# Moving 32 conditioning columns out of the latent attention's heads, and adding their biases eight at a time

## The chip, the cores and the metric

The kernel runs on one core of a Trainium2 chip. The metric is device time in microseconds (us). One core has a matrix engine (TensorE, PE; its weight loads are PEld), a vector engine (VectorE, DVE), an activation engine (ScalarE, ACT), a general engine (GpSimd, POOL), and a queue that issues most transfers (SyncE, SP). Each engine runs its own instructions in the order in which they were queued, and waits on semaphores for the others.

## The reference, cut to what matters

A network of two blocks works on 512 tokens of width 1024, in 32-bit floats. Each of its three layers is steered by a conditioning vector of 6 x 1024 numbers, cut into shifts, scales and gates:

```
c_act = silu(c)
for i in range(2):
    mod = c_act @ w_ada[i] + b_ada[i]            # 1024 x 6144
    sh1, sc1, g1, sh2, sc2, g2 = split(mod, 6)
    h = rmsnorm(x, mix_norm[i]) * (1 + sc1) + sh1
    y = fox_mixer(h) if i == 0 else mla_mixer(h)  # 16 heads each, causal
    x = x + g1 * y
    h = rmsnorm(x, ffn_norm[i]) * (1 + sc2) + sh2
    x = x + g2 * hier_moe(h)                      # 16 experts
mod = silu(c2) @ cond_w + cond_b                  # for the second block
...                                               # convolution, recurrence, PEER experts
```

Both mixers end with an output projection of 1024 x 1024. Nothing but `mod` of the second block needs the third conditioning vector.

## The kernel before

**Conditioning columns.** A vector `mod` is held as 48 columns of 128 numbers (8 columns for each of its six parts). One column is a row block of the transposed weight, 128 x 1024 floats (512 KB), loaded by SP into a tile `ada_w`. One DVE instruction multiplies it by the broadcast `silu` row and sums along the row (line 182, with a short read of the accumulator behind it), and one more DVE instruction adds the bias of that column (queued at line 184, run from line 168, so the profile shows it as L168, 128 x 1). The tiles come from a ring of three buffers in whichever pool `self.ring` names; the generator keeps one tile ahead of the column at work.

The first 16 columns of layer 0 are made at the start. The other 128 (32 of layer 0, 48 of layer 1, 48 of the second block) form one generator, `aside`, made in `run`. `step(n)` takes n columns from it. `heads` calls it: `steps` gives, for each quarter of the 16 heads, the columns taken per head. Before, the first attention takes (3, 4, 4, 8) per head, 76 columns, and the latent attention (2, 2, 2, 7), 52. The row `silu` has one buffer: `silu_row` for the second block (line 152 loads it through SP, line 153 applies the function on ACT) comes when column 80 has been used.

**Attention.** `heads` runs the two attentions alike. Four heads form a quarter; `quart` projects a quarter's queries, keys and values ahead of the heads that use them (`proj_tok`, three matmuls by `mm3`, lines 124 to 126). A head makes scores on PE, then a chain for each of four row blocks: maximum on DVE (L318), exponential on ACT (L321), reciprocal and scaling on DVE (L323, L325), transpose on PE (L334), copy on ACT (L335), and at last the product with the values (L352) whose copy by ACT (L353) ends the head. Two heads are interleaved. In the latent attention POOL also scales and rotates queries and keys (L748, L594 to L599, L772).

**Output projection.** `out_proj` splits the attention's output into a high and a low part (L535, L536), and makes eight chunks: a weight tile (L117 on ACT, L118 on DVE), 24 matmuls, and the update of x on DVE (L551); `then` adds the expert router's work for the chunk before. The expert layer's first weights are requested through SP while this runs.

**Order.** A scheduler at compile time orders each engine's queue by a model of the durations, by priority in the order of the program: what is ready is taken early where an engine has room. Tile pools are stacked from the left or the right of the on-chip memory, and a tile that overlaps an older one waits until that one has been used.

Of the kernel before, what the change touches and what calls it, by code (L numbers as in the profile page):

```python
# [15 lines left out]
OP = mybir.AluOpType  # L16
# [9 lines left out]
class Net:  # L26
    def __init__(self, nc, tc, ctx, A, out, dbg=None):
        self.nc, self.tc, self.ctx, self.A, self.out = nc, tc, ctx, A, out
        self.dbg = dbg or {}
        self.ring, self.more, self.over, self.extra, self.turn, self.ahead = None, None, None, {}, {}, {}  # L30

        self.holds, self.hold = [], None
        ec = ctx.enter_context
        self.cp = ec(tc.tile_pool(name="const", bufs=1))
        self.wp = ec(tc.tile_pool(name="wstream", bufs=1))
        self.xp = ec(tc.tile_pool(name="resid", bufs=1))
        self.sm = ec(tc.tile_pool(name="small", bufs=2))
        self.dram = ec(tc.tile_pool(name="dram", bufs=1, space=bass.MemoryType.DRAM))
        self.ps_acc = ec(tc.tile_pool(name="ps_acc", bufs=1, space=PSUM))
        self.ps = None  # L40
        self.consts()
# [111 lines left out]
        nc.scalar.activation(s, s, AF.Silu)  # L153
        return s

    def ada(self, c, w, mod, cols, how="V", bufs=3, lag=2):

        nc = self.nc  # L160
        V = nc.vector
        mod, bias = mod
        cols = list(cols)
        rs, late = [], []

        def total(to):
            while late and late[0][0] <= to:
                late.pop(0)[1]()  # L168

        for k, i in enumerate(cols):  # L170
            total(k)
            while len(rs) < min(k + bufs - 1, len(cols)):
                r = self.ring.tile([128, D], F32, tag="ada", bufs=bufs, name="ada_w")
                nc.sync.dma_start(out=r, in_=w[cols[len(rs)]])
                rs.append(r)
            r = rs[k]
            m = self.small([128, 1], "ada_t", bufs=8)
            if how[k % len(how)] == "S":
                nc.gpsimd.tensor_tensor(r, r, c, op=OP.mult)
                late.append((k + lag, functools.partial(nc.scalar.activation, r, r, AF.Copy, accum_out=m)))  # L180
            else:
                V.scalar_tensor_tensor(r, r, 1.0, c, op0=OP.mult, op1=OP.mult, accum_out=m)  # L182
            e = slice(i, i + 1)
            late.append((k + lag, functools.partial(V.tensor_tensor, mod[:, e], bias[:, e], m, op=OP.add)))
            if k == len(cols) - 1:
                total(k + lag)
            yield

    def step(self, n):
        for _ in range(n):  # L190
            next(self.aside)


# [161 lines left out]
    def heads(self, quart, oT, pool, steps, early, first):  # L355

        nc = self.nc
        ready, run = [], []  # L360

        pt = pool.tile([128, 13, 128], F32, name="pt")

        def fill():
            for q in range(4):
                yield from quart(q, ready)
            while True:
                yield

        self.ring = pool  # L370
        more = fill()
        while not ready:
            next(more)
            next(first, None)
        for _ in first:
            pass
        for _ in range(early):
            next(more)
        for head in range(16):
            r0 = (head % 2) * 64  # L380
            run.append(self.head(ready.pop(0), oT[r0:r0 + 64, head // 2, :], pt, pool))
            last = head == 15
            for k in range(4 if not last else 12):
                for g in reversed(list(run)):
                    if next(g, run) is run:
                        run.remove(g)
                if k != 3:
                    next(more)
                n = steps[head // 4]
                self.step((k + 1) * n // 4 - k * n // 4 if k < 4 else 0)  # L390
            while not ready and not last:
                next(more)
        self.ring = None
# [47 lines left out]
    def fox_heads(self, h, oT, keep, pool):  # L441
        nc, A = self.nc, self.A
        cq = keep.tile([128, 4, 512], BF16, name="f_cq")
        ck = keep.tile([128, 4, 512], BF16, name="f_ck")
# [67 lines left out]

            return score, v[:, :, hh * 64:(hh + 1) * 64]

        self.heads(quart, oT, pool, (3, 4, 4, 8), 1, self.fox_cum(h, cq, ck, oT[:, 2:8], keep))

    def proj_tok(self, ps, h, ws, i):

# [19 lines left out]

    def out_proj(self, x, oT, w, g1, pool, then=None):

        nc = self.nc
        o = self.split(oT, pool, "o")
        for c in range(8):
            wt = self.weight(w[c])
            ps = self.psum("acc", 2)
            for kd in range(8):
                e = slice(kd * 128, (kd + 1) * 128)
                self.mm3(ps, (wt[0][:, e], wt[1][:, e]), (o[0][:, kd, :], o[1][:, kd, :]), kd == 0, kd == 7)
            if then and c:
                then(c - 1)  # L550
            nc.vector.scalar_tensor_tensor(x[:, c, :], ps, g1[:, c:c + 1], x[:, c, :], op0=OP.mult, op1=OP.add)  # L551
        if then:
            then(7)

# [171 lines left out]
    def mla_heads(self, lat, cs, oT, pool):  # L726
        nc, A = self.nc, self.A
        V = nc.vector
        cq, ckv, gq, gk, kss, kr, rest = lat
# [60 lines left out]

            return score, vs[:, :, hh * 64:(hh + 1) * 64]

        self.heads(quart, oT, pool, (2, 2, 2, 7), 2, rest)


    def first_max(self, x, n, k, pool, name):
# [386 lines left out]
    def mla_layer(self, x, mod, cs, stack, then):  # L1183

        with self.pool("m_o") as po:
            oT = po.tile([128, 8, 512], F32, name="oT")
            with self.pool("m_lat") as pl:
                with stack, self.room:
                    lat = self.mla(x, cs, oT, pl)
                with self.pool("m_heads") as p:  # L1190
                    self.mla_heads(lat, cs, oT, p)
            self.cond.close()
            with self.pool("m_out") as p:
                self.out_proj(x, oT, self.A["mla_w_out"], mod[:, 16:24], p, then=then())


    def add_sums(self, sums, x, c, n):
# [612 lines left out]
    def peer_pick(self, h, keep, pool, ahead):  # L1810
# [21 lines left out]
        first = pool.tile([128, 16], BF16, name="first")  # L1832
        step = pool.tile([128, 16], F32, name="step")
        nc.gpsimd.memset(step, 0.0)
        for r0, n, w, at in self.CAND:
            for r in range(r0, r0 + n):
# [323 lines left out]
    def run(self):  # L2160
        nc, A = self.nc, self.A
        self.cond = contextlib.ExitStack()
        cond = self.cond.enter_context(self.pool("cond", "right"))
        act = self.silu_row(A["c"], cond)
        x = self.xp.tile([128, 8, 512], F32, name="x")
        nc.sync.dma_start(out=x, in_=A["x"])
        gain = self.xp.tile([128, 4, 8], F32, name="gain")
        nc.gpsimd.dma_start(out=gain, in_=A["norms"])
        gm, gf = gain[:, 0:2], gain[:, 2:4]
        bias = self.bias = self.xp.tile([128, 3, 48], F32, name="bias")  # L2170
        nc.scalar.dma_start(out=bias, in_=A["b_ada"])
        mods = [self.xp.tile([128, 48], F32, name=f"mod{k}") for k in range(3)]

        def aside():
            for k in range(3):
                c = self.silu_row(A["c2"], cond) if k == 2 else act
                yield from self.ada(c, A[f"w_ada{k}"], (mods[k], bias[:, k]), range(0 if k else 16, 48))

        self.aside = aside()
        loads = [self.moe_loads(l) for l in range(2)]  # L2180
        with self.psum_pool("ps") as self.ps:
            stack = [contextlib.ExitStack() for _ in range(2)]
            start = [functools.partial(self.moe_begin, stack[l], x, gf[:, l], mods[l], loads[l]) for l in range(2)]
            self.fox_layer(x, gm[:, 0], act, mods[0], start[0])
            self.moe_layer(0, x, gf[:, 0], mods[0], lambda room: self.mla_begin(room, x, gm[:, 1], mods[1]))
            self.mla_layer(x, mods[1], self.cs, stack[0], start[1])
            self.moe_layer(1, x, gf[:, 1], mods[1], lambda room: self.second_begin(x))
            self.room.close()
            stack[1].close()
            mod = mods[2]  # L2190
            self.second_mix(x, mod)
        self.peer_layer(x, mod)
# [107 lines left out]
```

## Time and profile before

| | us |
|---|---|
| median of 3 runs | 3050.35 (3048.65 to 3057.16) |
| the profiled execution, device time | 3048.28 |
| its span, first to last instruction | 3046.4 |
| PE busy | 2748.0 (90%) |
| DVE busy | 2342.8 (77%) |
| ACT busy | 1400.3 (46%) |
| POOL busy | 1235.6 (41%) |

Busy times are sums over the whole span; stages differ, so they are read by stretches. [...] In a timeline a line is start, duration, engine, source line, operation, output from input, and in brackets how long the engine was idle before it and what ended that.

### The profile page before, as it was taken

What the parts mean: (1) busy time and instruction counts of PE and PEld (TensorE: products, weight loads), DVE (VectorE), ACT (ScalarE), POOL (GpSimd) and SP (SyncE); (2) the same over time, 40 slices, a digit from 0 to 9 for tenths busy, and PEclk for the clock granted to TensorE, in tenths of its full rate; (3) what the DMA queues carried; (4) which work ended last, traced back from release to release, by engine and by line L of the source; (5) the groups of instructions that cost most, each with busy time, mean ns of one, the idle gap of its engine ahead of it and who ended that gap; (6) DMA issues with size and microseconds to landing.
All of it is one profiled execution on the core that took longest, in us unless ns stands there. A gap on an engine that the chain in (4) does not pass through costs nothing.

```text
span 3046.4 us, 42674 instructions
## 1 busy us (share of the span) xinstructions
PE 2748.0 (90%) x14989; PEld 2234.8 (73%) x14989; DVE 2342.8 (77%) x4500; ACT 1400.3 (46%) x2688; POOL 1235.6 (41%) x894
## 2 busy tenths in 40 slices
PE   2899978898889798899898899999899999999996
PEld 2777556676556566576676588999889999998885
DVE  7998457768974686777974699998598888886667
ACT  3354437744554574432333533688533333333332
POOL 3111017743211484004941245120177777774332
PEclk9999889999899799998998999999999999999998
DMA  6776158933634797221011124796699999997782
GB/s 217 245 231 198 42 212 293 330 132 125 190 126 151 244 341 241 90 73 28 5 59 57 69 83 128 228 316 219 214 363 350 351 356 351 349 351 270 247 265 98
DMA packets 234337, 627.53 MB, mean 206 GB/s; under 512 B 33180, under 2 KB 95948, under 8 KB 230648
## 3 DMA queue, kind: packets, MB, share of 16 engines
q1 hardware_dynamic: 134416, 434.54, 42.0%
q0 software_dynamic: 45120, 154.42, 14.4%
q10 hardware_dynamic: 54568, 35.66, 4.0%
q8 instruction: 122, 2.00, 0.3%
q14 instruction: 111, 0.91, 0.1%
HBM read 564.94 MB, written 63.37 MB: 206 GB/s over the span
## 4 chain that ended last, share of the span: by engine, by line
PE 47%; DVE 13%; DMA 3%; issue 2%; ACT 1%; POOL 0%; POOLq 0%; DVEq 0%; ACTq 0%; SPq 0%
PE acc L124 7%; PE acc L125 7%; PE acc L126 7%; PE y L126 6%; PE y L125 6%; PE y L124 5%; DVE s_y L1367 1%; DMA wraw<-in_moe_w_gu_dram 1%; PE S L1922 1%; PE tr L1922 1%; DVE wlo L118 1%; DMA wraw<-in_moe_w_dn_dram 1%; DVE s_y L1526 1%; DVE wc L1550 1%; DVE t L1774 1%
## 5 line engine op out<-in xcount | busy, mean ns | idle before, releaser
L118 DVE TENSOR_TENSOR wlo<-wraw,whi 128x1024 fp32r<-128x1024 f32 x442 | 620.2, 1414 | 202.9 <-ACT whi L117 198.7
L117 ACT ACTIVATE whi<-wraw 128x1024 fp32r<-128x1024 f32 (+1 forms) x552 | 576.6, 1050 | 415.8 <-PE acc L125 254.3
L124 PE MATMUL acc<-h_hi,whi 128*128 128x384 f32 (+1 forms) x1328 | 475.8, 359 | 12.2 <-ACT z_out L1962 7.5
L126 PE MATMUL acc<-h_hi,wlo 128*128 128x384 f32 (+1 forms) x1328 | 466.6, 351 | 2.2 <-DVE wlo L118 2.2
L125 PE MATMUL acc<-h_lo,whi 128*128 128x384 f32 (+1 forms) x1328 | 468.1, 353 | 0.0
L118 POOL TENSOR_TENSOR wlo<-wraw,whi 128x1024 fp32r<-128x1024 f32 (+1 forms) x110 | 278.8, 2542 | 325.8 <-ACT whi L117 317.7
L124 PE MATMUL y<-whi,hid_h 128*128 128x512 f32 x768 | 299.8, 391 | 8.0 <-ACT hid_h L2059 8.0
L126 PE MATMUL y<-whi,hid_l 128*128 128x512 f32 x768 | 303.0, 395 | 4.2 <-DVE hid_l L2060 4.2
L125 PE MATMUL y<-wlo,hid_h 128*128 128x512 f32 x768 | 302.4, 394 | 0.0
L1994 POOL DMA_INDIRECT gu<-in_peer_u_dram,e x128 | 196.0, 1531 | 243.2 <-DVE gu L2003 172.5
L124 PEld LDWEIGHTS acc<-h_hi,whi 128*128 128x128 f32 x1328 | 251.5, 190 | 30.4 <-ACT z_out L1962 8.4
L126 PEld LDWEIGHTS acc<-h_hi,wlo 128*128 128x128 f32 x1328 | 251.1, 189 | 16.7 <-DVE wlo L118 2.5
L1994 POOL DMA_INDIRECT gv<-in_peer_v_dram,e x128 | 200.1, 1563 | 155.1 <-DVE stage L1927 105.6
L125 PEld LDWEIGHTS acc<-h_lo,whi 128*128 128x128 f32 x1328 | 251.5, 189 | 15.7 <-issue 0.8
L2059 ACT ACTIVATE hid_h<-hid 128x384 fp32r<-128x384 f32 x128 | 67.1, 524 | 286.6 <-PE y L125 263.5
L2035 DVE SCALAR_TENSOR_TENSOR y<-gv,pz,y 128x1024 f32<-128x1024 f32 x128 | 183.5, 1434 | 0.7 <-DMA gv<-in_peer_v_dram,e 0.6
L182 DVE SCALAR_TENSOR_TENSOR ada_w<-ada_w,silu 128x1024 f32<-128x1024 f32 x138 | 174.3, 1263 | 7.8 <-DMA ada_w<-in_w_ada_dram 7.8
L124 PEld LDWEIGHTS y<-whi,hid_h 128*128 128x128 f32 x768 | 145.0, 189 | 38.0 <-ACT hid_h L2059 8.4
L126 PEld LDWEIGHTS y<-whi,hid_l 128*128 128x128 f32 x768 | 145.1, 189 | 33.9 <-DVE hid_l L2060 4.6
L125 PEld LDWEIGHTS y<-wlo,hid_h 128*128 128x128 f32 x768 | 145.0, 189 | 31.1 <-DVE wlo L118 0.3
L2003 DVE SCALAR_TENSOR_TENSOR gu<-gu,hrow 128x1024 f32<-128x1024 f32 x128 | 162.7, 1272 | 5.4 <-DMA gu<-in_peer_u_dram,e 5.4
L124 PE MATMUL acc<-whi,h_hi 128*128 128x256 f32 x480 | 140.6, 293 | 28.4 <-ACT whi L117 18.7
(671 smaller groups left out, 6231.5 us busy)
## 6 DMA issues: line engine op xcount, KB each, us to landing
ada_w<-in_w_ada_dram SPq DMA_DIRECT2D x144, 512.0 KB
wraw<-in_moe_w_gu_dram SPq DMA_DIRECT2D x128, 512.0 KB
wraw<-in_peer_ut_dram SPq DMA_DIRECT2D x128, 512.0 KB
wraw<-in_peer_v_dram SPq DMA_DIRECT2D x128, 512.0 KB
wraw<-in_moe_w_dn_dram SPq DMA_DIRECT2D x64, 512.0 KB
p_gd<-stage SPq DMA_DIRECT2D x24, 1024.0 KB
gt<-p_gd ACTq DMA_DIRECT2D x16, 1536.0 KB
wraw<-in_fox_w_in_dram SPq DMA_DIRECT2D x24, 512.0 KB
```

What stands on the lines that cost most here:

```text
L117: nc.scalar.activation(hi[:, :w], r[:, :w], AF.Copy)
L118: self.low = eng.tensor_tensor(lo[:, :w], r[:, :w], hi[:, :w].bitcast(F32), op=OP.subtract).ins
L124: mm(out=out, lhsT=l[0], rhs=r[0], start=start, stop=False)
L125: mm(out=out, lhsT=l[0], rhs=r[1], start=False, stop=False)
L126: mm(out=out, lhsT=l[1], rhs=r[0], start=False, stop=stop)
L182: V.scalar_tensor_tensor(r, r, 1.0, c, op0=OP.mult, op1=OP.mult, accum_out=m)
L1367: V.scalar_tensor_tensor(acc[:, c, :], *tap(n), acc[:, c, :], op0=OP.mult, op1=OP.add)
L1922: nc.tensor.matmul(out=pt[:, t * 128:(t + 1) * 128], lhsT=a2[:, b * 4 + t, :], rhs=a1[:, b * 4 + t, :], start=True, stop=True)
L1994: nc.gpsimd.indirect_dma_start(out=u, out_offset=None, in_=src[:, :], in_offset=bass.IndirectOffsetOnAxis(ap=e3[:, k:k + 1], axis=0))
L2003: V.scalar_tensor_tensor(u, u, 1.0, hrow, op0=OP.mult, op1=OP.mult, accum_out=z8[b][:, k % 8:k % 8 + 1])
L2035: V.scalar_tensor_tensor(y3, vs.pop(k), z8[k // 8][:, k % 8:k % 8 + 1], y3, op0=OP.mult, op1=OP.add)
L2059: nc.scalar.activation(hh, hid, AF.Copy)
```

## The change

The columns are taken at other places: (3, 4, 4, 12) per head in the first attention (92 columns), two in each of the first four chunks of its output projection (8), (0, 1, 1, 3) per head in the latent attention (20), and two in each of the first four chunks of its output projection (8). So 32 columns leave the latent heads: 16 go to the last quarter of the first attention's heads, 16 to the two output projections.

With `whole`, the sums of eight columns are collected in one tile of 128 x 8 and their biases added by one instruction: 16 adds in place of 128. Where a stage ends, the last step loads no tile ahead (`prefetch`), so that the ring of one pool holds no column of the next; `out_proj` therefore begins with two loads of its own. The pool `cond`, which holds the `silu` row, is stacked from the left in place of the right, and lives until the latent output projection is done; the ring adds three tiles of 4 KB a partition to the pools of the output projections.

```diff
-    def ada(self, c, w, mod, cols, how="V", bufs=3, lag=2):
+    def ada(self, c, w, mod, cols, how="V", bufs=3, lag=2, whole=False):
...
-            while len(rs) < min(k + bufs - 1, len(cols)):
+            while len(rs) < min(k + (bufs - 1 if self.prefetch else 1), len(cols)):
...
-            m = self.small([128, 1], "ada_t", bufs=8)
+            if whole:
+                if i % 8 == 0:
+                    sums = self.small([128, 8], "ada_s", bufs=3)
+                m = sums[:, i % 8:i % 8 + 1]
+            else:
+                m = self.small([128, 1], "ada_t", bufs=8)
...
-            e = slice(i, i + 1)
-            late.append((k + lag, functools.partial(V.tensor_tensor, mod[:, e], bias[:, e], m, op=OP.add)))
+            if not whole:
+                e = slice(i, i + 1)
+                late.append((k + lag, functools.partial(V.tensor_tensor, mod[:, e], bias[:, e], m, op=OP.add)))
+            elif i % 8 == 7:
+                e = slice(i - 7, i + 1)
+                late.append((k + lag, functools.partial(V.tensor_tensor, mod[:, e], bias[:, e], sums, op=OP.add)))
...
-    def step(self, n):
-        for _ in range(n):
+    def step(self, n, last=False):
+        for k in range(n):
+            self.prefetch = not last or k < n - 1
             next(self.aside)
...
-                self.step((k + 1) * n // 4 - k * n // 4 if k < 4 else 0)
+                self.step((k + 1) * n // 4 - k * n // 4 if k < 4 else 0, last and k == 3)
...
-        self.heads(quart, oT, pool, (3, 4, 4, 8), 1, self.fox_cum(h, cq, ck, oT[:, 2:8], keep))
+        self.heads(quart, oT, pool, (3, 4, 4, 12), 1, self.fox_cum(h, cq, ck, oT[:, 2:8], keep))
...
         o = self.split(oT, pool, "o")
+        self.ring = pool
         for c in range(8):
...
+            if c < 4:
+                self.step(2, c == 3)
             if then and c:
...
-        self.heads(quart, oT, pool, (2, 2, 2, 7), 2, rest)
+        self.heads(quart, oT, pool, (0, 1, 1, 3), 2, rest)
...
-            self.cond.close()
             with self.pool("m_out") as p:
                 self.out_proj(x, oT, self.A["mla_w_out"], mod[:, 16:24], p, then=then())
+        self.cond.close()
...
-        cond = self.cond.enter_context(self.pool("cond", "right"))
+        cond = self.cond.enter_context(self.pool("cond"))
...
-                yield from self.ada(c, A[f"w_ada{k}"], (mods[k], bias[:, k]), range(0 if k else 16, 48))
+                yield from self.ada(c, A[f"w_ada{k}"], (mods[k], bias[:, k]), range(0 if k else 16, 48), whole=True)
```

## Rows read from the trace of the kernel before

**Rows 1.** Windows, all engines, by stage: stretch, length, busy (count), clock, DMA share, GB/s.

```profile
145.00:296.00 151.00, 150.22 (x1027) 120.09 (x1026) 136.99 (x380) 76.58 (x185) 19.48 (x18) 1.00 0.69 224
...
313.00:371.00 58.00, 54.29 (x207) 29.43 (x208) 26.50 (x66) 31.10 (x81) 5.16 (x5) 0.79 0.00 1
375.00:418.00 43.00, 43.00 (x177) 29.60 (x175) 20.83 (x20) 15.28 (x18) 11.87 (x5) 1.00 0.60 207
711.00:757.50 46.50, 34.47 (x156) 26.19 (x154) 43.51 (x111) 21.92 (x51) 18.53 (x13) 0.89 0.43 136
757.50:803.90 46.40, 38.64 (x175) 25.91 (x175) 45.30 (x118) 24.95 (x68) 23.00 (x16) 0.89 0.55 171
803.90:889.90 86.00, 72.56 (x328) 46.27 (x328) 77.84 (x229) 47.00 (x126) 15.35 (x10) 0.88 0.58 183
889.90:934.80 44.90, 40.16 (x192) 22.48 (x192) 19.04 (x54) 26.79 (x74) 0.00 (x0) 0.96 0.25 83
938.00:990.00 52.00, 52.00 (x203) 35.11 (x201) 27.72 (x29) 19.16 (x25) 11.11 (x6) 1.00 0.47 156
```

**Rows 2.** Windows of line 182 alone, columns and accumulator reads: DVE busy (count).

```profile
757.50:803.90 46.40, 17.17 (x25) 0.89 0.55 171
803.90:889.90 86.00, 38.30 (x64) 0.88 0.58 183
```

**Rows 3.** Windows of line 168 alone, bias adds: DVE busy (count), ACT busy (count).

```profile
757.50:803.90 46.40, 5.73 (x13) 0.00 (x0) 0.89 0.55 171
803.90:889.90 86.00, 12.36 (x33) 0.00 (x0) 0.88 0.58 183
```

**Rows 4.** Timelines of POOL and of DVE around 773, latent heads.

```profile
772.14 3.67 POOL L772 TENSOR_TENSOR rk<-rk,qk_r_y 128x1536 f32<-128x1536 f32 x1 [7.06 <-DVE qk_r_y L144]
...
773.19 2.63 DVE L168 TENSOR_TENSOR mod<-bias,ada_t 128x1 f32<-128x1 f32 x1
```

**Rows 5.** Waits of PE from 757.5 to 889.9: us, times, longest.

```profile
PE tr L334 <- DVE P L325: 12.3, 4, 3.6
```

**Rows 6.** ACT timeline: ends of latent heads 3, 10 and 15.

```profile
803.87 0.59 ACT L353 ACTIVATE oT<-pv 64x512 f32<-64x512 f32 x1
...
889.86 0.59 ACT L353 ACTIVATE oT<-pv 64x512 f32<-64x512 f32 x1 [0.37 <-PE pv L352]
...
934.75 0.59 ACT L353 ACTIVATE oT<-pv 64x512 f32<-64x512 f32 x1 [5.03 <-PE pv L352]
```

**Rows 7.** PE timeline: every third matmul of a projection, two widths.

```profile
761.48 0.34 PE L126 MATMUL acc<-whi,lat_l 128*128 128x384 f32 x1
...
762.01 0.34 PE L126 MATMUL acc<-whi,lat_l 128*128 128x384 f32 x1
...
787.10 0.40 PE L126 MATMUL acc<-whi,lat_l 128*128 128x512 f32 x1
...
787.80 0.40 PE L126 MATMUL acc<-whi,lat_l 128*128 128x512 f32 x1
```

**Rows 8.** Line 126 from 803.9 to 889.9: one of the three matmul lines of a projection.

```profile
L126 PE MATMUL acc<-whi,lat_l x24: 336/368/397, 804.2 to 861.6; 128*128 128x512 f32 x12, 128*128 128x384 f32 x12
```

**Rows 9.** DVE groups from 76 to 298: busy us, mean ns, idle before.

```profile
L182 DVE SCALAR_TENSOR_TENSOR ada_w<-ada_w,silu 128x1024 f32<-128x1024 f32 x77 | 94.8, 1231 | 6.8 <-DMA ada_w<-in_w_ada_dram 6.8
...
L168 DVE TENSOR_TENSOR mod<-bias,ada_t 128x1 f32<-128x1 f32 x77 | 10.9, 146 | 0.0
```

**Rows 10.** ACT timeline of the latent attention: function and table load.

```profile
728.14 1.06 ACT L153 ACTIVATE silu<-silu 128x1024 f32<-128x1024 f32 x1 [0.84 <-DMA silu<-in_c_dram]
...
744.90 1.28 ACT L321 ACT_TABLE_LOAD   x1
746.20 0.37 ACT L321 ACTIVATE P<-S,sm_mx 128x128 f32<-128x128 f32 x1
```

**Rows 11.** SP queue: loads of the first expert layer's weights.

```profile
370.56 2.30 SPq L105 DMA_DIRECT2D wraw<-in_moe_w_gu_dram  x5
...
424.09 42.00 SPq L105 DMA_DIRECT2D wraw<-in_moe_w_dn_dram  x2
```

More of the change, by code (lines that the diff above doesn't have):

```diff
@@ L29, in __init__ @@
         self.dbg = dbg or {}
-        self.ring, self.more, self.over, self.extra, self.turn, self.ahead = None, None, None, {}, {}, {}
+        self.ring, self.prefetch, self.more, self.over, self.extra, self.turn, self.ahead = None, True, None, None, {}, {}, {}
         self.holds, self.hold = [], None
@@ L551, in out_proj @@
             nc.vector.scalar_tensor_tensor(x[:, c, :], ps, g1[:, c:c + 1], x[:, c, :], op0=OP.mult, op1=OP.add)
+        self.ring = None
         if then:
```

## The prediction

> **What bounds the kernel now.** I read the windows by stage first, then the windows of the column work alone, the timelines of DVE and POOL in the latent heads, and last the ends of the heads.
>
> In the first attention's steady stretch PE is busy 150.2 of 151.0 us at full clock, with DVE at 137.0 [rows 1]: PE sets the pace, a busy DVE costs nothing. In its last heads, 313 to 371, DVE is busy only 26.5 of 58.0 us, and no column is left there: the scheduler has pulled them all forward. [...] The latent heads are the other way round. From 757.5 to 889.9 DVE is busy 45.3 of 46.4 and 77.8 of 86.0 us, PE 38.6 and 72.6, clock 0.89 and 0.88 [rows 1]. Columns are a large part of that DVE time: 17.2 and 38.3 us for line 182 [rows 2], 5.7 and 12.4 us for the bias adds [rows 3]. Without both, DVE would be busy 22.4 of 46.4 and 27.2 of 86.0. PE does wait for DVE: 12.3 us in four waits for the scaled `P` [rows 5]. The last five latent heads have no columns: PE 40.2 of 44.9, DVE 19.0, clock 0.96 [rows 1].
>
> A bias add is dear in the latent heads. In the first attention one takes 146 ns [rows 9]; at 773.19 one takes 2.63 us, ending with the 3.67 us POOL instruction that began before it [rows 4], and everything queued on DVE behind it waits too. The 46 of [rows 3] cost 18.1 us, 393 ns each.
> [...]
>
> **The change, part by part.**
>
> *Latent heads, second stretch, 803.9 to 889.9.* This holds seven heads, 803.87 to 889.86, and the five that follow end at 934.75 [rows 6]: 12.3 us a head against 9.0. It also holds projections: 12 matmuls of each width on each of three lines [rows 8], so 36 of each. Three of 384 columns take 0.53 us and three of 512 take 0.70 [rows 7]: 6.4 + 8.4 = 14.8 us. Seven heads at 9.0 plus 14.8 are 77.7 us, 8 below the 86.0. Were the projections also to fill PE's idle time as the last five heads show it (4.7 us in five heads, 6.6 in seven [rows 1]), it would be 71, a gain of 15. Which columns leave? Before, 13 run in 757.5 to 803.9 and 32 in this stretch (25 and 64 instructions, two to a column) [rows 2], so 7 run earlier, of 52. The scheduler pulls columns forward as soon as it can, so I expect the 20 that stay to be the first 20, done by about 804, and this stretch to lose its columns wholly. I take 10, between 8 and 15; the low bound is 0, should PE's waits there come from something else.
>
> *First stretch, 757.5 to 803.9.* It keeps most of its columns, but the adds shrink from 13 to one or two, 5 us of DVE in a stretch that is 98% full. Three heads at 9.0 and some 10 us of projections (the other half of a quarter's and a bit) would need 37 of the 46.4, so the gain lies between 0 and 9. I take 4. *Front, 711 to 757.5:* DVE 43.5 of 46.5 [rows 1], again a few adds fewer; 0 to 5, I take 2. The latent heads together: -16, bounds 0 and -29.
>
> *First attention, 16 more columns.* One column costs 1.23 us [rows 9] and its 0.08 us read of the accumulator: 21 us. The 77 bias adds of 10.9 us [rows 9] become nine or ten, which frees some 7 us of DVE in 145 to 296, beside its 14 us of idle time there [rows 1]. So about as much room appears as the new columns need, and part of them will run while PE is the bound, at no cost, hidden by 150.2 us of PE work. I let half of them fall behind 296, in a chain where PE waits for the maximum and the scaling. Eight instructions of 1.23 us, each delaying a chain of two interleaved heads by a third of its length: +3. Bounds 0 and 16 x 1.23 = 20.
>
> *The silu row moves too.* Column 80 now falls into the first attention, so the second row's load and function run there, in the midst of exponentials. The function takes 1.06 us, a table load 1.28 [rows 10]. Before, the function needed no load of its own, since the expert layer had left its table; now one load goes ahead of it and one behind it: 1.06 + 2 x 1.28 = 3.6 us on ACT, which the softmax chain waits for. Taken at +2, for PE has the other head; bounds 0 and 3.6.
> [...]
>
> *Output projections, eight columns each.* PE is busy all of 43.0 and all of 52.0 us, DVE 20.8 and 27.7 [rows 1]. Eight columns add 10.5 us to a DVE with 22 and 24 idle. Weight parts are prepared ahead and the update of x has the next chunk's matmuls as cover, so I take +1 each, +2; bounds 0 and, if each column held PE for its length, 20. Their 4.2 MB of loads go through SP, among the expert weights. A column load that waits for a ring tile holds those weights behind it, and the expert layer's first matmuls wait for them. Cover: from 375 to 418 transfers take 0.60 of the engines for 207 GB/s, so eight loads need 12 us of such time, and 17 are free [rows 1]. Besides, the queue itself stands for up to 42 us from 424.09 with its buffers full [rows 11]. Taken at 0; 12 us a layer if that cover were gone. The loads that begin each output projection wait for no data but memory, and find a DVE with other work; 0. The pool's change of side moves 4 KB from one end to the other: 0, with the same cover if it delays an expert tile. The first attention's saved adds lie under PE's work: 0, at most a gain of the 10.9.
>
> *Sum*, on the profiled execution's 3048.3 (span 3046.4 and 1.9 around it): 3048.3 - 16 + 3 + 2 + 2 = 3039.3. The median of the runs is 2.1 above that execution, so the predicted gain is 9 us on its own base, 11 on the median's. About 0.3%, 9 us, is what a measurement can tell from no change: below 3041.2 is faster, above 3059.5 slower.
>
> **The rivals.** *More:* the latent heads fall to PE's own rate in all three stretches, -26, and the new columns hide, +4: 3026. For it: DVE 32% busy without columns in the second stretch, and a clock of 0.96 where none run. Against it: 20 columns and all of POOL's work stay. *Paid back:* the latent heads wait as much for POOL and for chains between ACT and PE as for DVE, and only the adds' waits go, -4; with +7 for the moved work, 3051. For it: only 12.3 us of PE's waits there name the scaled `P` [rows 5]. Against it: that DVE is 91 to 98% full. *Slower:* the moved columns break the chain in 313 to 371 and PE's clock falls. There 54.3 us of PE at 0.79 [rows 1] are 42.9 at full clock; at 0.50 they are 86, +31, so 3048.3 - 16 + 2 + 2 + 31 = 3067. It decides from a granted clock of about 0.55 there (+24, 3060). Against it: DVE has 31 idle us and transfers stand still. *No move at all:* the scheduler may run the 16 in the PE-bound stretch; that only makes the +3 vanish.
>
> **How the numbers follow.** Forecast, 3031 to 3045: 0.44, of which 0.31 below 3041.2. More: 0.21. Paid back, 3045 to 3059: 0.22. Slower: 0.13. Faster is 0.31 + 0.21 = 0.52, no change 0.13 + 0.22 = 0.35, slower 0.13. The predicted time is 3039; the range, 3020 to 3060, goes down to the more of the latent heads' bounds (-29 and small costs) and up to where the slower case begins.
>
> **What would show it.** In the new profile: the latent heads 4 to 10 take 11 us each or less, with no line 182 in them and a clock above 0.88; DVE there is about a third busy; the bias adds are 16 with a total under 10 us; the first attention's last heads end 2 to 7 us later, with one function and two table loads on ACT among them; the output projections keep PE full, and the first expert matmul comes no later after the projection than before. The prediction is wrong if the columns that stay spread over all latent heads, if the waits for DVE are replaced by waits for POOL, or if the clock in the last heads of the first attention drops.

## The result and the profile after

The changed kernel takes 3096.06 us (median of 4 runs, 3088.87 to 3099.59) against 3049.5 (4 runs, 3046.99 to 3057.16): a ratio of 1.0135 [1.011, 1.016], slower, where 3039 was forecast. The span of its profiled execution is 3093.3 us against 3046.4.

I first set the windows of the new trace beside [rows 1], each stretch cut at the same instructions (end of the same head, the same update of x), but for the front, whose row here begins 6 us earlier in its stage than that of [rows 1]. The stretches are: the first attention's steady part, its last heads, its output projection, the latent attention's front to the end of head 0, heads 1 to 3, 4 to 10 and 11 to 15, and its output projection. Columns as in [rows 1]; clock is the mean granted clock of PE in the stretch, as a share of the full one.

```profile
151.00:303.40 152.40, 152.37 (x1033) 121.70 (x1033) 137.10 (x345) 77.50 (x187) 25.85 (x18) 1.00 0.72 237
319.40:380.50 61.10, 54.00 (x210) 28.75 (x210) 27.95 (x71) 27.42 (x74) 6.14 (x5) 0.78 0.11 36
388.00:431.00 43.00, 43.00 (x168) 29.20 (x167) 23.85 (x34) 10.13 (x13) 0.00 (x0) 1.00 0.51 163
728.00:793.00 65.00, 44.50 (x179) 32.54 (x178) 58.22 (x143) 25.64 (x63) 28.64 (x20) 0.84 0.49 156
793.00:831.00 38.00, 34.14 (x170) 22.86 (x171) 31.29 (x91) 22.03 (x59) 10.52 (x9) 0.96 0.41 124
831.00:913.00 82.00, 73.94 (x336) 46.33 (x335) 44.45 (x140) 48.99 (x132) 13.34 (x10) 0.92 0.05 13
913.00:958.50 45.50, 40.54 (x188) 23.15 (x187) 15.84 (x48) 26.02 (x72) 0.00 (x0) 0.92 0.10 35
962.00:1014.00 52.00, 51.89 (x201) 34.77 (x199) 29.59 (x44) 12.18 (x18) 1.17 (x2) 1.00 0.52 181
```

The latent heads did what was meant: 38.0 and 82.0 us in place of 46.4 and 86.0. The windows of the columns alone (now line 188: DVE busy, count) answer to [rows 2]: none is left behind head 3.

```profile
793.00:831.00 38.00, 12.27 (x18) 0.96 0.41 124
831.00:913.00 82.00, 0.00 (x0) 0.92 0.05 13
```

But the front of that stage grew: from one and the same instruction it takes 65.1 us in place of 52.8. Whole stretches that lie between these rows grew too. The table gives the length of seven stages, from the starts of the same instructions in each kernel's trace; below the first line, the difference to it. **First head**: from the span's start to the copy that ends head 0 of the first attention. **Heads**: from there to the copy of head 15. **Out, router**: to the first copy of gathered rows in the expert layer. **Front**: from the last row of the latent projection to the end of latent head 0. **Latent heads**: to head 15. **Out, router 2**: as the first. **Last**: from the first to the last copy of hidden values in the second block's retrieval experts. What lies between (the experts, the second block) differs by less than 6 us each. Each row is one execution: those of pad96 and held_no_out are the slowest of their ten, those of e1_eights, held_wide, held_wide_mod and pad64 the fastest, so a row tells where the time went, and the medians below how much a kernel takes.

| us | first head | heads | out, router | front | latent heads | out, router 2 | last |
|---|---|---|---|---|---|---|---|
| before | 145.1 | 225.5 | 88.1 | 52.8 | 177.2 | 90.7 | 806.6 |
| **after** | +5.9 | +3.7 | +14.1 | +12.3 | -11.8 | +10.9 | +10.0 |
| e1_eights | +6.4 | -2.4 | +0.4 | +0.5 | +3.8 | -0.2 | +9.6 |
| e2_single | +0.4 | +7.0 | +14.3 | +8.3 | -17.7 | +10.7 | +0.1 |
| e3_no_out | +6.5 | +4.5 | +0.9 | +13.6 | -11.8 | +1.5 | +9.9 |
| e6_out_alone | +6.0 | -0.9 | +15.6 | +13.3 | -14.7 | +10.0 | +11.7 |
| n_no_loads | -0.7 | +9.7 | +13.0 | +10.4 | -21.5 | +9.8 | +3.5 |
| m_ring_two | +1.1 | +2.1 | +0.6 | +9.5 | -13.3 | +0.2 | +5.6 |
| h_held | -0.7 | +4.1 | +0.4 | -5.2 | -12.1 | -0.2 | +0.0 |
| held_again | -0.5 | +7.9 | +0.7 | -3.9 | -15.8 | +0.5 | +3.1 |
| held_wide_mod | +6.3 | -0.7 | +1.0 | -3.8 | -9.2 | -0.8 | +0.5 |
| held_wide | +5.6 | +0.8 | +0.5 | -3.8 | -9.1 | -0.1 | +9.7 |
| held_no_out | +0.7 | +6.8 | +0.5 | -0.1 | -6.7 | -0.5 | +14.4 |
| pad96 | +1.7 | +1.2 | -0.1 | -0.1 | -0.5 | +0.2 | +15.4 |
| pad64 | -0.5 | -0.1 | -0.4 | -1.7 | -2.7 | -0.9 | -0.7 |
| pad32 | -0.3 | +0.5 | +0.2 | -0.2 | -3.0 | -0.2 | +9.0 |

The line of the changed kernel adds up to 45.1 of the 46.9 us between the two spans. Four places lose; each is read in the trace before the runs are told.

**First head.** The SP queue of the changed kernel, then that of the kernel before, as the second quarter's weights come up:

```profile
88.85 20.49 SPq L175 DMA_DIRECT2D ada_w<-in_w_ada_dram  x10
110.88 1.54 SPq L105 DMA_DIRECT2D wraw<-in_fox_w_in_dram  x2
```

```profile
88.76 9.32 SPq L174 DMA_DIRECT2D ada_w<-in_w_ada_dram  x5
100.89 0.33 SPq L105 DMA_DIRECT2D wraw<-in_fox_w_in_dram  x1
```

Ten column loads now stand in one piece ahead of the next weights, which are requested at 110.88 in place of 100.89, though this part takes the same columns as before.

**Output projection and router.** The same queue around the end of the first attention (380.04), to be read against [rows 11]:

```profile
305.36 87.23 SPq L175 DMA_DIRECT2D ada_w<-in_w_ada_dram  x16
393.40 0.33 SPq L105 DMA_DIRECT2D wraw<-in_fox_w_out_dram  x1
396.32 0.33 SPq L175 DMA_DIRECT2D ada_w<-in_w_ada_dram  x1
399.28 0.33 SPq L105 DMA_DIRECT2D wraw<-in_fox_w_out_dram  x1
404.83 24.66 SPq L105 DMA_DIRECT2D wraw<-in_moe_w_gu_dram  x12
...
460.84 5.72 SPq L105 DMA_DIRECT2D wraw<-in_moe_w_dn_dram  x2
466.69 2.67 SPq L105 DMA_DIRECT2D wraw<-in_moe_w_gu_dram  x4
```

The first load of expert weights goes out at 404.83, 24.8 us behind the end of the attention; before, at 370.56 with the attention's end at 370.53. The twelve stand behind the last projection weight, where before they stood between. They don't go out together either. Four of them wait, at 404.83, 411.64, 418.39 and 425.15, for the splits (L118) of the last four projection weights, and the other eight follow these from 425.54. The queue's waits from 400 to 430:

```profile
SPq L105 <- DVE wlo L118: 24.2, 4, 6.4
```

The loads behind the twelve are late in turn: those of 460.84 and 466.69 were out by 419.59 before, and now they move while the router gathers its rows. A wait of the changed kernel in that stretch, the same wait before, and two windows after:

```profile
PE tr L1001 <- DMA hg<-rows,lst: 16.1, 1, 16.1
```

```profile
PE tr L984 <- DMA hg<-rows,lst: 9.7, 1, 9.7
```

```profile
440.00:450.00 10.00, 4.22 (x16) 2.97 (x16) 8.85 (x24) 3.26 (x8) 4.68 (x3) 0.50 1.01 399
...
470.00:480.00 10.00, 0.03 (x1) 0.06 (x1) 0.00 (x0) 0.00 (x0) 1.26 (x2) 0.50 0.91 288
```

From 470 to 480 PE stands still with the transfers 0.91 busy: it waits for gathered rows, whose transfers take 26.4% of the 16 transfer engines' time in that window beside 64.5% for the queue with the late weights. What that wait grew by, 9.7 to 16.1, is 6.4 of the 14.1 us. The first gather is also issued 8.3 us later, counted from the attention's end (469.1 against 451.3); where that comes from I haven't traced.

**Latent front.** DVE after, in the key norm of the first quarter (`qk_v` to the last `qk_r_y`), and POOL's scaling of the keys that waits for it:

```profile
749.17 1.22 DVE L188 SCALAR_TENSOR_TENSOR ada_w<-ada_w,silu 128x1024 f32<-128x1024 f32 x1
...
750.32 1.78 DVE L786 TENSOR_SCALAR qk_v<-qk_ss 128x16 f32<-128x16 f32 x1
...
755.53 1.21 DVE L188 SCALAR_TENSOR_TENSOR ada_w<-ada_w,silu 128x1024 f32<-128x1024 f32 x1
...
759.35 1.82 DVE L188 SCALAR_TENSOR_TENSOR ada_w<-ada_w,silu 128x1024 f32<-128x1024 f32 x1
...
764.35 0.55 DVE L756 TENSOR_REDUCE qk_ss<-qk_sq 128x4 f32<-128x384 f32 x1 [2.68 <-ACT qk_sq L755]
...
767.59 0.17 DVE L144 SCALAR_TENSOR_TENSOR qk_r_y<-qk_r_z,qk_r_y 128x16 f32<-128x16 f32 x1
```

```profile
767.83 3.77 POOL L789 TENSOR_TENSOR rk<-rk,qk_r_y 128x1536 f32<-128x1536 f32 x1 [6.20 <-DVE qk_r_t L139]
```

The norm is a chain of twelve tiny instructions. Here it takes from 750.32 to 767.59, 17.3 us, with two columns inside it, one ahead, and the next quarter's projection work between its steps. The two columns are 3.0 us of that themselves; the rest of what it lost is that work, waits, and slower steps (one of 2.33 us against 0.70). Before, the chain took 6.2 us and no column stood in it: `qk_v` at 729.12, the last step at 735.33, the next column at 735.42:

```profile
729.12 0.16 DVE L769 TENSOR_SCALAR qk_v<-qk_ss 128x16 f32<-128x16 f32 x1
...
735.33 0.17 DVE L144 SCALAR_TENSOR_TENSOR qk_r_y<-qk_r_z,qk_r_y 128x16 f32<-128x16 f32 x1
735.42 1.22 DVE L182 SCALAR_TENSOR_TENSOR ada_w<-ada_w,silu 128x1024 f32<-128x1024 f32 x1
```

**Last.** The second block is not touched. Yet in 400 us of its last stage PE, never idle and at full clock in both kernels, gets through 2013 matmuls after and 2028 before (windows of the changed kernel, then of the kernel before). This is told with the last experiments.

```profile
2340.00:2740.00 400.00, 400.00 (x2013) 361.21 (x2012) 331.18 (x379) 141.47 (x201) 289.84 (x199) 1.00 0.97 349
```

```profile
2300.00:2700.00 400.00, 400.00 (x2028) 363.90 (x2027) 333.69 (x380) 142.48 (x203) 290.61 (x201) 1.00 0.97 351
```

### The profile page after: what moved, and what is told of

Read it like the earlier page. It is cut to its first block, busy times and chain, and to the rows that moved or that the text cites. A ratio compares the mean times of both kernels' runs of the same rounds, so it can differ in the third digit from the quotient of the medians.

```text
span 3093.3 us, 42580 instructions
## 1 busy us (share of the span) xinstructions
PE 2773.0 (90%) x14989; PEld 2242.4 (72%) x14989; DVE 2334.7 (75%) x4388; ACT 1402.3 (45%) x2690; POOL 1222.6 (40%) x894
## 3 DMA queue, kind: packets, MB, share of 16 engines
q0 software_dynamic: 45120, 154.42, 14.3%
## 4 chain that ended last, share of the span: by engine, by line
PE 47%; DVE 13%; DMA 3%; issue 1%; ACT 1%; POOL 0%; POOLq 0%; ACTq 0%; DVEq 0%; SPq 0%
PE acc L124 7%; PE acc L125 7%; PE acc L126 7%; PE y L126 6%; PE y L125 6%; PE y L124 6%; DMA wraw<-in_moe_w_gu_dram 2%; DVE s_y L1384 2%; PE tr L1939 1%; PE S L1939 1%; DVE wlo L118 1%; DVE s_y L1543 1%; DMA wraw<-in_moe_w_dn_dram 1%; DVE wc L1567 1%; DVE t L1791 1%
## 5 line engine op out<-in xcount | busy, mean ns | idle before, releaser
L118 DVE TENSOR_TENSOR wlo<-wraw,whi 128x1024 fp32r<-128x1024 f32 x442 | 610.6, 1392 | 211.6 <-ACT whi L117 208.5
L118 POOL TENSOR_TENSOR wlo<-wraw,whi 128x1024 fp32r<-128x1024 f32 (+1 forms) x110 | 275.0, 2506 | 207.5 <-ACT whi L117 188.7
```

The lines of the kernel that those rows point to most:

```text
L118: self.low = eng.tensor_tensor(lo[:, :w], r[:, :w], hi[:, :w].bitcast(F32), op=OP.subtract).ins
```

## The experiments

Each is timed against the kernel before on its chip (medians there 3049.8 to 3055.5). A line of "..." in a diff leaves lines out.

**Which part of the change.** *e1_eights* is the kernel before with the adds in eights. Against the changed kernel (the pool `cond` is on its old side too):

```diff
-        self.heads(quart, oT, pool, (3, 4, 4, 12), 1, self.fox_cum(h, cq, ck, oT[:, 2:8], keep))
+        self.heads(quart, oT, pool, (3, 4, 4, 8), 1, self.fox_cum(h, cq, ck, oT[:, 2:8], keep))
...
-            if c < 4:
-                self.step(2, c == 3)
...
-        self.heads(quart, oT, pool, (0, 1, 1, 3), 2, rest)
+        self.heads(quart, oT, pool, (2, 2, 2, 7), 2, rest)
```

> The columns stay where they were before; only the biases are added eight at a time. Theory 'adds': the front loss comes from this part, because with fewer vector instructions in the program's model ten column loads are queued together ahead of the first attention's next weights: head 0 of the first attention ends about 6 us later than before, the first expert layer's router stage takes the same time as before (0 to 2 us), and the whole stands 0 to 6 us above the kernel before, since the latent heads may give back some of the 18 us that their single adds cost. Rival 'moves': the adds are innocent, head 0 ends as before and the whole is 5 to 15 us faster.

3070.56 us, ratio 1.006 [1.0036, 1.0084]. The first head's loss is here, +6.4, with the same ten loads ahead of the weights, and nothing at either router (+0.4, -0.2). But the whole is 20.8 us above the kernel before where at most 6 were expected: +9.6 in the last stage, and the latent heads got 3.8 slower for all the adds they are rid of.

*e2_single* leaves out `whole=True` alone:

```diff
-                yield from self.ada(c, A[f"w_ada{k}"], (mods[k], bias[:, k]), range(0 if k else 16, 48), whole=True)
+                yield from self.ada(c, A[f"w_ada{k}"], (mods[k], bias[:, k]), range(0 if k else 16, 48))
```

> All columns are moved as in the changed kernel, but each bias is added by itself. Theory 'queue' (the output projections' column loads hold the expert weights back): head 0 ends as before, each of the two router stages still takes about 10.6 us more, and the whole is 3080 to 3092. Rival 'adds': the wide adds and the schedule that they bring are the cause of most of it, and the whole is within 10 us of the kernel before.

3079.15 us, 1.0082 [1.0054, 1.011], 1 us under the expected. First head +0.4 and last stage +0.1, so these two come with the wide adds; +14.3 and +10.7 at the routers, so these do not. The latent heads gain 17.7, with the front still 8.3 late.

*e3_no_out* puts the output projections' columns into the last latent quarter:

```diff
-        self.ring = pool
...
-            if c < 4:
-                self.step(2, c == 3)
...
-        self.heads(quart, oT, pool, (0, 1, 1, 3), 2, rest)
+        self.heads(quart, oT, pool, (0, 1, 1, 7), 2, rest)
```

> As the changed kernel, with the wide adds, 92 columns in the first attention and its lower cond pool, but the 16 columns of the output projections go to the last quarter of the latent heads (7 a head). Theory 'queue': both router stages return to their length of before (0 to 2 us more in place of 10.6 each), and the whole is 3070 to 3078, or up to 10 more if the latent heads pay for the 16 columns. Rival 'placement' (the cond pool on the other side and held longer delays expert tiles) or 'first attention' (its tail and the second row): the router stages keep their 10.6 us each, and the whole stays above 3088.

3071.04 us, 1.0063 [1.0043, 1.0082]. The routers are back (+0.9, +1.5) although `cond` lies on its new side: its place is not the cause. The front keeps its 13.6.

*e6_out_alone* keeps the output projections' columns and gives the first attention its old ones:

```diff
-        self.heads(quart, oT, pool, (3, 4, 4, 12), 1, self.fox_cum(h, cq, ck, oT[:, 2:8], keep))
+        self.heads(quart, oT, pool, (3, 4, 4, 8), 1, self.fox_cum(h, cq, ck, oT[:, 2:8], keep))
...
-        self.heads(quart, oT, pool, (0, 1, 1, 3), 2, rest)
+        self.heads(quart, oT, pool, (0, 1, 1, 7), 2, rest)
```

> As the changed kernel, but the first attention keeps its 76 columns, so only the output projections take columns from the latent heads (16). Theory 'queue': the router stages keep about 10 us more each, the first attention's tail loses its extra 3 us, head 0 still ends 6 us later; the whole is 3084 to 3096. Rival 'first attention': the 16 columns in its last heads and the second row are what delays the stages behind it, and the whole is under 3070.

3097.29 us, 1.0139 [1.0096, 1.0183], 1 us above the expected: as slow as the whole change, +15.6 and +10.0 at the routers, and the first attention's heads without their loss.

**Queue or memory at the router.** So eight columns in an output projection hold the expert weights back. By their loads, which stand in the queue, or by their ring, whose 12 KB a partition reach above the bottom of the pool in which the expert weights land? *n_no_loads* takes away the loads and leaves the ring, so 16 columns are left out of its result; *m_ring_two* leaves the loads and cuts the ring to 8 KB, which ends below that pool. Both from e2_single:

```diff
                 r = self.ring.tile([128, D], F32, tag="ada", bufs=bufs, name="ada_w")
-                nc.sync.dma_start(out=r, in_=w[cols[len(rs)]])
+                if not self.inout:
+                    nc.sync.dma_start(out=r, in_=w[cols[len(rs)]])
...
-                V.scalar_tensor_tensor(r, r, 1.0, c, op0=OP.mult, op1=OP.mult, accum_out=m)
+                V.scalar_tensor_tensor(r, c if self.inout else r, 1.0, c, op0=OP.mult, op1=OP.mult, accum_out=m)
```

> As e2_single (all columns moved, biases added singly), but the output projections' 16 columns are not loaded: each multiplies the silu row by itself into its ring tile, so those 16 columns of the conditioning are left out of the result. The vector work and the ring's 12 KB of memory stay, the loads in the queue go. Theory 'queue': with no column load ahead of them, the expert weights are requested as early as before (first one right after the first attention's end, about 8 us behind its last head's load of before), and both router stages return to their old length; the whole loses some 20 us against e2_single. Rival 'memory': the ring overlaps the lowest tiles of the expert weights' pool, so these are still requested only behind the whole output projection (about 30 us later than before), and both router stages keep some 10 us more; the whole stays within 6 us of e2_single.

```diff
-                r = self.ring.tile([128, D], F32, tag="ada", bufs=bufs, name="ada_w")
+                r = self.ring.tile([128, D], F32, tag="ada", bufs=2 if self.inout else bufs, name="ada_w")
```

> As e2_single, but the ring of the output projections has two tiles instead of three, so that it ends below the pool of the expert weights; all loads stay in the queue, each tile one turn later. Theory 'queue': the loads still hold the weights back, at least as much as before, and the whole is 3079 or more. Rival 'memory': the expert weights are requested between the column loads, the router stages lose most of their 10 us each, and the whole is 3055 to 3066.

The two SP queues, n_no_loads first:

```profile
392.78 5.09 SPq L105 DMA_DIRECT2D wraw<-in_fox_w_out_dram  x2
404.21 24.75 SPq L105 DMA_DIRECT2D wraw<-in_moe_w_gu_dram  x12
```

```profile
373.74 0.33 SPq L105 DMA_DIRECT2D wraw<-in_moe_w_gu_dram  x1
375.49 0.33 SPq L175 DMA_DIRECT2D ada_w<-in_w_ada_dram  x1
375.91 0.38 SPq L105 DMA_DIRECT2D wraw<-in_moe_w_gu_dram  x1
```

Without any column load the weights are as late as ever, at 404.21, and the routers keep +13.0 and +9.8 (3074.18 us, 1.0065 [1.0041, 1.0088]). With the loads between them but a ring of two, the first weight goes out at 373.74 and both routers are back, +0.6 and +0.2 (3058.13 us, 1.0003 [0.9979, 1.0027]). My theory that the column loads hold the weights back falls: it is the ring's third tile. In the built kernels it lies at bytes 152640 to 156736 of a partition, and the first weight of the first expert lands at 153120 to 157216; a ring of two ends at 152544.

The trace doesn't show that weight waiting for the tile, though. The last column is read by 403.05, and eight of the twelve weights go out from 425.54. What the overlap changes is the order of the queue, which is fixed at compile time. In the changed kernel and in n_no_loads the third expert's four weights, which land in the buffers of the projection's own weights and so wait for their splits, stand ahead of those of the first two experts; in the kernel before and in m_ring_two they stand behind them. Why the scheduler turns the order round no run here shows.

**The latent front.** *h_held* queues the latent columns behind the last step of the first key norm, on m_ring_two:

```diff
+            self.newton = V.scalar_tensor_tensor(y, z, 1.5, y, op0=OP.add, op1=OP.mult).ins
...
+                with self.tc.issue_after(self.keyed) if self.keyed else contextlib.nullcontext():
+                    V.scalar_tensor_tensor(r, r, 1.0, c, op0=OP.mult, op1=OP.mult, accum_out=m)
...
+            self.keyed = self.keyed or self.newton
```

> As m_ring_two, and the latent heads' columns are queued on the vector engine behind the last step of the first key norm. Theory 'chain': the first latent head ends 8 to 13 us earlier against the start of its stage than in m_ring_two, since three columns no longer stand between the steps of that norm; the later heads keep their gain, and the whole is 6 to 13 us below m_ring_two. Rival 'elsewhere': the norm is late for its projections or for the general engine, and the hold changes less than 3 us.

3046.25 us, 0.9966 [0.9942, 0.999]. The front goes from +9.5 to -5.2, and the heads keep -12.1. In its DVE timeline the chain is short again, 728.56 to 736.27, and the first column stands behind it:

```profile
728.56 0.17 DVE L788 TENSOR_SCALAR qk_v<-qk_ss 128x16 f32<-128x16 f32 x1
...
736.27 0.17 DVE L145 SCALAR_TENSOR_TENSOR qk_r_y<-qk_r_z,qk_r_y 128x16 f32<-128x16 f32 x1
736.35 1.22 DVE L190 SCALAR_TENSOR_TENSOR ada_w<-ada_w,silu 128x1024 f32<-128x1024 f32 x1
```

> The same kernel as h_held, timed in more rounds beside the next three. If its gain is real it lies 5 to 16 us below the kernel before again, with an interval that stays below 1; if it was a lucky set of runs, the interval takes in 1.

3046.24 us against 3050.46, 0.9986 [0.9972, 1.0]: 4.2 us below, with an interval that reaches 1, so it just misses both signs of a real gain. The trace shows the latent stage 19.7 us shorter again (-3.9 and -15.8) and 7.9 of it lost in the first attention's heads. The gain in device time is 9 us in the first measurement and 4 in the second, at the limit of what they tell.

*held_no_out* has the single adds and the hold, but 36 columns in the latent heads and none in the output projections (and `cond` on its old side):

```diff
-        self.heads(quart, oT, pool, (0, 1, 1, 3), 2, rest)
+        self.heads(quart, oT, pool, (2, 2, 2, 3), 2, rest)
```

> Single adds and the held columns, but no columns in the output projections: 92 in the first attention and 36 in the latent heads (2, 2, 2, 3). If the output projections' columns are free once the ring is short, this is 5 to 10 us slower than h_held, since 16 more columns run in the latent heads; if they still cost there, it is as fast or faster.

3055.24 us, 1.0006 [0.9986, 1.0026]: the front and heads gain 6.8 in place of 17.3 and 19.7. With a short ring the output projections' columns are nearly free, as the +0.6 and +0.2 of m_ring_two say too.

**The wide adds and the last stage.** *held_wide_mod* and *held_wide* put `whole=True` back into h_held, the first with the sums in place:

```diff
-                if i % 8 == 0:
-                    sums = self.small([128, 8], "ada_s", bufs=3)
-                m = sums[:, i % 8:i % 8 + 1]
+                m = mod[:, i:i + 1]
```

> As h_held, but the biases are added eight at a time, with the eight sums kept in the columns of the modulation vector themselves, so that no tile is added and no address moves. Theory 'order': the wide adds alone bring the ten column loads ahead of the first attention's third pair of weights, head 0 ends 5 to 7 us later than in h_held, the last stage takes the same time, and the whole is 4 to 10 us above h_held. Rival 'address': what the wide adds cost comes with the 96 bytes; head 0 ends within 2 us of h_held, and so does the whole.

> As held_wide_mod, but with the tiles of eight sums as in the changed kernel (96 bytes a partition more): this is the changed kernel with a ring of two in the output projections and the held columns, nothing else. Theory 'address': its front is that of held_wide_mod within 1 us, and it is 5 to 12 us slower, most of it in the last stage. Rival: the last stage's length changes from run to run and not with the addresses; the two kernels' medians are within 4 us.

3053.74 (1.0013 [0.9996, 1.0031]) and 3059.81 (1.0029 [1.0016, 1.0042]). In both the first head is about 6 us late, so this loss comes with the wide adds and not with the addresses. Only the second, with 96 bytes more among the small tiles, loses in the last stage (+9.7 against +0.5; the medians lie 6.1 us apart). *pad96*, *pad64* and *pad32* give the kernel before nothing but such a tile:

```diff
+        pad = self.sm.tile([128, 24], F32, tag="pad", bufs=1, name="pad")
+        nc.gpsimd.memset(pad, 0.0)
```

> The kernel before with 96 bytes a partition more in the pool of small tiles, which is what the collected sums take in the changed kernel; nothing else but one fill of that tile. Theory 'address': the last stage (the second block's retrieval experts) takes about 10 us more, as in all four kernels with wide adds, and the whole is about 3060. Rival 'adds': the shift does nothing, and the last stage takes its old time, within 1 us.

> The kernel before with 64 bytes a partition more in the pool of small tiles. Theory 'address': whether the last stage is slow hangs on where its tiles lie within some step of addresses; a shift by 64 bytes is one of the two that tell the step, and with pad32 at least one of the two takes 9 to 16 us more in that stage. Rival 'run': the stage's time changes from run to run by itself (0 to 14 us in the unshifted kernels so far), and both kernels' medians lie within 4 us of the kernel before.

> The kernel before with 32 bytes a partition more in the pool of small tiles. Theory 'address': as for pad64; if the step is 64 bytes, this one is slow like pad96 (9 to 16 us more in the last stage) and pad64 is not. Rival 'run': within 4 us of the kernel before, like pad64.

3063.14 (1.003 [1.0011, 1.005]), 3048.86 (0.9983 [0.9969, 0.9997]) and 3057.51 (1.0011 [0.9996, 1.0027]); last stage +15.4, -0.7, +9.0. One group of its matmuls over 400 us, in pad64 and in pad32 (busy, mean ns, idle):

```profile
L126 PE MATMUL y<-whi,hid_h 128*128 128x512 f32 x288 | 112.0, 389 | 0.0
```

```profile
L126 PE MATMUL y<-whi,hid_h 128*128 128x512 f32 x288 | 113.5, 394 | 0.0
```

It is 388 ns in the kernel before and 395 in the changed one; the two other lines of this product differ less, 392 and 394 ns before, 394 and 396 after. A shift by 64 bytes is harmless, by 32 or 96 it costs 9 us or more in these traces; the medians of pad32 and pad64, timed side by side, lie 8.7 us apart. But that is not all: the unshifted kernels lie between 0 and +5.6, and held_no_out, unshifted too, at +14.4 with 397 ns in that group. A part changes without any shift (h_held +0.0 and held_again +3.1 are one kernel), and why stays open. So does pad64's 0.9983: a tile that should do nothing moves a ratio by 0.002, so no ratio as near to 1 says much.

## Why the prediction was wrong

**The step that failed** is the output projections' expert weights, "taken at 0; 12 us a layer if that cover were gone". The stages lost +14.1 and +10.9. That this lies near 12 is luck: the price was the transfer time of eight column loads, and the cover wasn't gone, since the transfers are 0.51 busy from 388 to 431 while the weights stand in the queue. I had asked whether the transfers find free time, and whether a load that waits holds the queue. I had not asked where the ring lies. The prediction weighs memory twice, for the loads that begin each output projection and for the pool that moves 4 KB, and passes over the 12 KB of the ring, which reach into the place of the first expert weight and turn the order of the queue round. n_no_loads and m_ring_two show that it is the ring's third tile, and not the column loads.

**The front** was -2, bounds 0 and -5; it became +12.3. I used the rule that the scheduler pulls columns forward wherever DVE has room, but not its other side: it pulls them into a chain on which POOL and PE wait. h_held shows that holding the columns back ends the loss. Why the old kernel was spared I can only argue: the second `silu` row was loaded and applied in the middle of this front [rows 10], so only four columns could come ahead of it. Every kernel that has that row earlier and no hold is 8.3 to 13.6 late here, every one that has it in the old place is within 1.7. No run has the old steps with an early row, so this rests on that split alone.

**The saved adds of the first attention** were 0 to a gain of 10.9; in every kernel with wide adds the first head is 5.6 to 6.5 us late. In all six traces ten column loads stand ahead of the next weights, and five in those with single adds. That these five more make the loss, and that the scheduler lets them go ahead because its model holds fewer instructions, is argued and not shown. In the latent heads, too, fewer adds brought nothing. In e1_eights, with all its columns in place, the two stretches of [rows 3] hold 2.6 us of adds in place of 18.1, and front and heads are 4.3 us longer. held_wide_mod's front and heads gain 13.0 where the two kernels with single adds gain 17.3 and 19.7. What eats it there I haven't traced. One held add stands in [rows 4]: 2.63 us against the 146 ns of [rows 9], with an end at 775.82 where a POOL instruction ends at 775.81. That POOL held it is read from the common end alone, and no run here shows that the time of the stage hung on such adds.

**The last stage** stood in no term: +10.0, most of it with the addresses (6 to 9 us by the medians).

**What was right.** The latent heads: -16 forecast for the whole stage, -17.3 and -19.7 once the front is left whole; in the changed kernel -11.8 behind a spoilt front. The columns that stay are the first ones, none behind head 3, and the bias adds take 0.3 us there, as forecast. The first stretch gave 8.4 in place of 4 in the changed kernel, but the second only 4.0 in place of 10, with heads 4 to 10 at 11.7 us each and DVE 54% busy, not a third. The first attention's 16 columns and the `silu` row: 3 + 2 forecast, +3.7 measured (+2.1 to +9.7 with single adds, -0.7 to +4.5 in the others with wide ones). Both table loads of the `silu` term stand in ACT's timeline, 1.28 us each, with the next function 0.02 and 0.01 us behind them, so the 3.6 us on ACT came as summed:

```profile
301.70 1.28 ACT L153 ACT_TABLE_LOAD   x1
303.00 1.06 ACT L153 ACTIVATE silu<-silu 128x1024 f32<-128x1024 f32 x1
...
308.34 1.28 ACT L333 ACT_TABLE_LOAD   x1
309.63 0.58 ACT L333 ACTIVATE P<-S,sm_mx 128x384 f32<-128x384 f32 x1
```

The output projections' own work: 2 forecast, 0.8 in m_ring_two. The rival that ended slower was not this one: the clock in the last heads is 0.78 against 0.79 before, far from 0.55. No run shows these heads at the mean of 0.50 in its sum, nor the 86 us of PE reckoned from it, which was an estimate; the trace of before has that clock from 430 to 460, where PE is busy 14.1 of 30 us.

By these runs the changed kernel's 45.1 us are: wide adds 6 in the first head and about 10 by addresses, the ring 25, the front 12, the first attention 4, less 12 in the latent heads.

## What to carry to other kernels

Before new tiles go into a stage, compare their place with the pools of what is loaded ahead for the next stage: a tile that overlaps them can push those loads back in the queue, here to 22 us past the tile's last use, and free transfer time (transfers 0.51 busy from 388 to 431) did not help. Where a scheduler fills gaps, work that becomes ready earlier goes into the gaps of dependent chains; look for what kept it out before, and tie it behind the chain if that goes away. Instructions taken off an engine that isn't waited for saved nothing here (from 76 us on, 77 adds of 10.9 us became 10 of 1.5 in the first attention, and its first head got 5.9 us longer), and can cost time where the queue order changes with them.

## What I had not expected of the hardware

PE's matmuls of the last stage, at full granted clock and never idle, take 388 to 389 ns in one group with the tiles where they were (the kernel before, e2_single, h_held) or 64 bytes on (pad64), and 394 to 395 with a shift of 32 or 96 bytes (pad32, pad96, the changed kernel), where that stage of 806.6 us is 9.0 to 15.4 us longer. Two executions without a shift show 391 ns (m_ring_two) and 397 ns (held_no_out) all the same, so the place isn't the only cause. What of the operands' place does it no run here shows.
